# Making the low part of every second half block of the up projection with ScalarE and an accumulating transfer

## The chip, the cores and the metric

The kernel runs on one core of a Trainium2 chip. Its engines are TensorE (PE; PEld is its weight load), VectorE (DVE), ScalarE (ACT), GpSimd (POOL) and SyncE (SP, which issues most transfers). The metric is the time of one execution in microseconds (us) as the device measures it, the median of several runs; lower is better.

## The reference

Two layers of an encoder on 256 tokens of width 2048, all in float32. What this change touches is the gated feed-forward part:

```python
h2 = rms_norm(x, ln2_g[l])
u = depthwise_conv(h2 @ w_up[l], conv_w[l], conv_b[l])     # w_up: 2048 x 11264
gate, up = u[..., :D_FF], u[..., D_FF:]                    # D_FF = 5632
x = x + (jax.nn.silu(gate) * up) @ w_down[l]
```

Before it each layer has an input projection, two attention groups and an output projection.

## The kernel before

Float32 products are made from parts. Each weight tile `w` and each activation is split into a high part `hi`, which is `w` rounded to the matmul's float32r type, and a low part `lo = w - hi`. For the up projection `two` issues for each block of 128 rows of weights one matmul of 512 columns (the high part of the weights times both parts of the activation, whose parts lie side by side) and one of 256 columns (the low part of the weights times the high part of the activation).

All weights come in blocks of 1 MB, the *quanta*: 128 partitions x 2048 floats. `load` fetches a block into one of three buffers `raw`, by a transfer on SP's queue. Each block is worked off in two halves of 128 x 1024, the *steps* `(q, half)`. `split_w(s)` takes a pair of buffers `whi`, `wlo` (five of each: SPLIT_AHEAD = 4, plus one) and calls `split`: ACT copies the half block to `whi` with rounding (L104), VectorE subtracts it from the original into `wlo` (L105). The main loop, for each step, splits the weights of four steps ahead and then issues the step's matmuls (L86). When both halves of a block are split, its `raw` buffer is given up and the load of the block three further on is issued.

A layer has 36 blocks of the input projection, 16 of the output projection, and in the feed-forward part 88 blocks of the up projection (two for each of 44 column blocks `f`) and 44 of the down projection. Up and down alternate: the up projection of 13 column blocks, then the down projection over 12 of them, then 12 more, and so on (CHUNKS). After the second block of an `f`, `glu` runs: ACT takes half of the result out of PSUM (L505), VectorE adds the other half and scales it into `halo` (L506, L507), POOL copies the edges of `halo` (L509, L510), ACT and VectorE do the conv of width 3 (L515, L517), ACT the SiLU (L519), VectorE the product (L520), and the split of the result into `mid`.

The order of instructions on each engine isn't written out by hand. A scheduler orders what the program records by priorities and by its own reckoning of times; `tc.high_priority` lets the splits go ahead of other work. The queues of the engines then run strictly in that order, with semaphores between them.

`lo` in a second half of the up projection is thus made by L105 on VectorE as everywhere else; POOL issues no transfers, and in the up projection it has only the two halo copies of each `f`.

Of the kernel before, what the change touches and what calls it, by code (L numbers as in the profile page):

```python
# [11 lines left out]
F32 = mybir.dt.float32  # L12
F32R = mybir.dt.float32r
I32 = mybir.dt.int32
AF = mybir.ActivationFunctionType
ALU = mybir.AluOpType
# [27 lines left out]
AHEAD_PRIO = 40  # L44
# [7 lines left out]
def encoder_kernel(  # L52
# [5 lines left out]
    nc = tc.nc  # L58
# [42 lines left out]
    def split(hi, lo, src, scale=None):  # L101

        if scale is None:
            high = nc.scalar.activation(hi, src, AF.Copy)  # L104
            nc.vector.tensor_sub(lo, src, hi.bitcast(F32))  # L105
        else:
            high = nc.scalar.activation(hi, src, AF.Copy, scale=scale)  # L107
            nc.vector.scalar_tensor_tensor(lo, src, scale, hi.bitcast(F32),
                                           op0=ALU.mult, op1=ALU.subtract)
        return high  # L110
# [266 lines left out]
    quanta = []  # L377
# [199 lines left out]
    raw, hl, left, loads, highs = {}, {}, {}, {}, {}  # L577

    def load(q, parts=1):
        if q < len(quanta):  # L580
            raw[q] = wp.tile([P, 2048], F32, name="raw", bufs=3)
            left[q] = 2
            m = 2048 // parts
            for j in range(parts):
                loads[q] = nc.sync.dma_start(out=raw[q][:, j * m:(j + 1) * m], in_=quanta[q][0][:, j * m:(j + 1) * m])

    def split_w(s, parts=1):
        if s < len(steps):
            q, half = steps[s]
            at_ = UP_AT if quanta[q][2] else 0  # L590
            hl[s] = tuple(wp.tile([P, 1024 + 64], F32R, name=t, bufs=SPLIT_AHEAD + 1)[:, at_:at_ + 1024]
                          for t in ("whi", "wlo"))
            m = 1024 // parts
            for j in range(parts):
                with tc.high_priority(offset=AHEAD_PRIO if s >= KD // 2 else 0):
                    highs[s] = split(*(t[:, j * m:(j + 1) * m] for t in hl[s]),
                                     raw[q][:, half * 1024 + j * m:half * 1024 + (j + 1) * m])
            left[q] -= 1
            if left[q] == 0:
                del raw[q]  # L600
                load(q + LOAD_AHEAD)
# [61 lines left out]
    for i in range(SPLIT_AHEAD):  # L663
        first_x(i)
        split_w(i, 2 if i == 0 else 1)
# [14 lines left out]
    for s, (q, half) in enumerate(steps):  # L680
        if s + SPLIT_AHEAD < KD // 2:
            first_x(s + SPLIT_AHEAD)
        split_w(s + SPLIT_AHEAD)
        quanta[q][1](q, half, *hl.pop(s))
        for f, args in side.pop((q, half), []):
            f(*args)
# [83 lines left out]
```

## Time and profile before

| | |
|---|---|
| time, median of 3 runs | 2126.05 us (2126.02 to 2126.58) |
| the profiled execution's own time | 2126.1 us |
| its span in the trace | 2124.3 us |
| granted TensorE clock | 1.00 |
| mean transfer rate over the span | 187 GB/s, 397.89 MB |

The profile is one execution. A group's row names the source line, the engine, the operation, the tile written and the tiles read, the shape and the number of instructions; behind the bar stand busy time in us, the mean of one in ns, and the idle time of the engine just before them with what ended most of it. A row of the timeline has the start in us, the duration in us, the engine and the operation, and in brackets the idle time before it. In the windows each engine's busy time stands in the order PE, PEld, DVE, ACT, POOL, and then the granted clock, the busy share of the DMA engines and GB/s.

### The profile page before, as it was taken

Reading aid. Unit: us, or ns where it says so; the run is one execution under the profiler, and the core shown is the slowest. Engines: PE = TensorE matmul, PEld = TensorE weight load, DVE = VectorE, ACT = ScalarE, POOL = GpSimd, SP = SyncE. Lnnn points to the kernel's source line nnn. Section 1 sums busy time; section 2 is a strip of 40 time slices with the busy share of each in tenths; the row PEclk is TensorE's granted clock in tenths of the full one; section 3 lists DMA queues with packets and bytes.
Section 4 is the critical chain, followed back from the end, with each engine's and each line's share of the span. In section 5 each row is a group of like instructions: output and inputs, shape, how many; then the busy total and the mean of one; then the engine's idle time right before and its main releaser. Section 6 shows DMA issues by size and latency. Waiting matters only on the chain.

```text
span 2124.3 us, 28802 instructions
## 1 busy us (share of the span) xinstructions
PE 2118.1 (100%) x10904; PEld 1815.3 (85%) x10904; DVE 1458.0 (69%) x2293; ACT 1141.2 (54%) x1651; POOL 142.1 (7%) x215
## 2 busy tenths in 40 slices
PE   9999999999999999999999999999999999999999
PEld 8888888888888888888888888888888888888887
DVE  7777667775677577657756866677756775776575
ACT  7566556554455355535655665565544553555453
POOL 0000000110011011001000000001100100110010
PEclk9999999999999999999999999999999999999999
DMA  9544555555555555555555454555555555555554
GB/s 345 195 141 170 176 178 178 181 197 198 181 196 191 189 195 182 196 198 182 196 180 197 139 171 160 174 182 185 197 194 184 195 188 192 193 185 197 192 185 139
DMA packets 60843, 397.89 MB, mean 187 GB/s; under 512 B 7328, under 2 KB 9888, under 8 KB 13728
## 3 DMA queue, kind: packets, MB, share of 16 engines
q1 hardware_dynamic: 59696, 394.71, 54.3%
q8 instruction: 85, 1.39, 0.3%
q10 hardware_dynamic: 1008, 1.34, 0.2%
q14 instruction: 54, 0.44, 0.1%
HBM read 393.93 MB, written 2.10 MB: 186 GB/s over the span
## 4 chain that ended last, share of the span: by engine, by line
PE 99%; DMA 0%; ACT 0%; DVE 0%; ACTq 0%; DVEq 0%; issue 0%
PE mm L86 95%; PE pv L86 1%; PE S L86 1%; PE tr L292 1%; PE S L140 0%; PE tr L353 0%; PE tr L86 0%; DMA ln_g<-in_ln_g 0%; PE tr L348 0%; PE tr L345 0%; DVE x L546 0%; ACT xs L107 0%; ACT whi L104 0%; ACTq L608 0%; DVEq L765 0%
## 5 line engine op out<-in xcount | busy, mean ns | idle before, releaser
L105 DVE TENSOR_TENSOR wlo<-raw,whi 128x1024 fp32r<-128x1024 f32 (+1 forms) x737 | 901.2, 1223 | 543.8 <-ACT whi L104 504.9
L104 ACT ACTIVATE whi<-raw 128x1024 fp32r<-128x1024 f32 (+1 forms) x737 | 779.7, 1059 | 863.1 <-PE mm L86 671.9
L86 PE MATMUL mm<-xs,whi 128*128 128x512 f32 x2816 | 976.6, 390 | 0.0
L86 PE MATMUL mm<-xs,wlo 128*128 128x256 f32 x2816 | 794.1, 282 | 0.0
L86 PEld LDWEIGHTS mm<-xs,whi 128*128 128x128 f32 x2816 | 528.3, 188 | 110.5
L86 PEld LDWEIGHTS mm<-xs,wlo 128*128 128x128 f32 x2816 | 532.2, 189 | 0.8
L86 PE MATMUL mm<-whi,mid 128*128 128x512 f32 x1920 | 481.5, 391 | 0.0
L86 PEld LDWEIGHTS mm<-whi,mid 128*128 128x128 f32 x1920 | 357.9, 188 | 72.7
L86 PE MATMUL mm<-whi,xs 128*128 128x512 f32 x1152 | 296.3, 395 | 0.7 <-ACT whi L104 0.7
L86 PE MATMUL mm<-wlo,mid 128*128 128x512 f32 x960 | 260.0, 390 | 0.0
L86 PEld LDWEIGHTS mm<-whi,xs 128*128 128x128 f32 x1152 | 214.6, 188 | 45.4 <-ACT whi L104 1.4
L86 PEld LDWEIGHTS mm<-wlo,mid 128*128 128x128 f32 x960 | 180.0, 188 | 37.2
L86 PE MATMUL mm<-wlo,xs 128*128 128x512 f32 x576 | 162.0, 396 | 0.0
L517 DVE SCALAR_TENSOR_TENSOR pT<-halo,conv,pT 128x256 f32<-128x256 f32 x352 | 146.7, 479 | 0.5
L86 PEld LDWEIGHTS mm<-wlo,xs 128*128 128x128 f32 x576 | 107.3, 188 | 21.7 <-DVE wlo L105 0.4
L509 POOL COPY halo<-halo 128x6 f32<-128x6 f32 x88 | 22.7, 258 | 1359.8 <-DVE halo L507 1359.8
L515 ACT ACTIVATE pT<-halo,conv 128x256 f32<-128x256 f32 x176 | 95.1, 588 | 0.2
L510 POOL COPY halo<-halo 128x6 f32<-128x6 f32 x88 | 95.1, 1081 | 0.2 <-POOL halo L509 0.2
L507 DVE TENSOR_TENSOR halo<-prob,r 128x512 f32<-128x512 f32 x88 | 60.9, 692 | 2.7
L506 DVE TENSOR_TENSOR prob<-prob,mm 128x512 f32<-128x512 f32 x88 | 59.9, 681 | 0.0
L453 DVE TENSOR_TENSOR x<-x,mm 128x1024 f32<-128x1024 f32 x28 | 34.2, 1221 | 35.3 <-PE mm L86 35.3
L505 ACT ACTIVATE prob<-mm 128x512 f32<-128x512 f32 x88 | 51.1, 581 | 0.0
(129 smaller groups left out, 857.8 us busy)
## 6 DMA issues: line engine op xcount, KB each, us to landing
raw<-in_w_up SPq DMA_DIRECT2D x176, 1024.0 KB, 4.8
raw<-in_w_down SPq DMA_DIRECT2D x88, 1024.0 KB, 4.8
raw<-in_w_in SPq DMA_DIRECT2D x71, 1024.0 KB, 4.9
raw<-in_w_out SPq DMA_DIRECT2D x32, 1024.0 KB, 4.8
bias<-in_bias SPq DMA_DIRECT2D x16, 160.0 KB, 3.8
x<-in_x SPq DMA_DIRECT2D x4, 512.0 KB, 8.9
out<-x SPq DMA_DIRECT2D x6, 256.0 KB, 2.5
mid<-in_xT ACTq DMA_DIRECT2D x4, 256.0 KB, 6.2
```

The lines of the kernel that those rows point to most:

```text
L86: nc.tensor.matmul(ps, lhsT, rhs, start=start, stop=stop, skip_group_check=True)
L104: high = nc.scalar.activation(hi, src, AF.Copy)
L105: nc.vector.tensor_sub(lo, src, hi.bitcast(F32))
L292: nc.tensor.transpose(ps[:, j, tt * P:(tt + 1) * P], qn[tt][:, p + j, :], ident)
L453: nc.vector.tensor_add(xv, xv, ps)
L505: nc.scalar.activation(t, ps[:, :, 0], AF.Copy)
L506: nc.vector.tensor_add(t, t, ps[:, :, 1])
L507: nc.vector.tensor_mul(ux[:, :, r:r + T], t, st["r2"][:, None, :].to_broadcast([P, 2, T]))
L509: nc.gpsimd.tensor_copy(ux[:, :, 1:r], ux[:, :, T:T + r - 1])
L510: nc.gpsimd.tensor_copy(ux[:, :, T + r:T + 2 * r - 1], ux[:, :, r + 1:2 * r])
L515: nc.scalar.activation(y[:, j, :], ux[:, j, r:r + T], AF.Identity, scale=w1, bias=b)
L517: nc.vector.scalar_tensor_tensor(y[:, j, :], ux[:, j, o:o + T], w, y[:, j, :], op0=ALU.mult, op1=ALU.add)
```

## The change

In `split_w`, for the second half (`half == 1`) of each block of the up projection, ACT makes the high part as before (now L599), then writes its negative into `lo` (L600), and POOL issues a transfer that reads the same half block of the weights a second time from memory and adds it to `lo` (L601). VectorE's subtraction is left out for these half blocks; the first halves and all other weights are split as before. Lines behind the insertion have numbers that are 9 higher.

```diff
             m = 1024 // parts
+            if quanta[q][2] and half == 1:
+
+                hi, lo = hl[s]
+                w = raw[q][:, 1024:2048]
+                with tc.high_priority(offset=AHEAD_PRIO):
+                    highs[s] = nc.scalar.activation(hi, w, AF.Copy)
+                    nc.scalar.activation(lo, hi.bitcast(F32), AF.Copy, scale=-1.0)
+                    nc.gpsimd.dma_start(out=lo, in_=quanta[q][0][:, 1024:2048], accum_op=ALU.add)
+                parts = 0
             for j in range(parts):
```

On ACT, in the middle of the first up projection, one turn of an `f` (`whi` and `wlo` are the parts of the weights, `prob`, `pT` and `mid` tiles of `glu`) stood before as

```order
L505 ACTIVATE prob<-mm 128x512
L104 ACTIVATE whi<-raw 128x1024
L515 ACTIVATE pT<-halo_110,conv 128x256 x2
L104 ACTIVATE whi<-raw 128x1024
L519 ACTIVATE prob<-pT 128x256
L104 ACTIVATE whi<-raw 128x1024
L104 ACTIVATE mid<-prob 128x256
L104 ACTIVATE whi<-raw 128x1024
```

and stands now as

```order
L505 ACTIVATE prob<-mm 128x512
L599 ACTIVATE whi<-raw 128x1024
L600 ACTIVATE wlo<-whi 128x1024
L515 ACTIVATE pT<-halo_110,conv 128x256 x2
L104 ACTIVATE whi<-raw 128x1024
L519 ACTIVATE prob<-pT 128x256
L599 ACTIVATE whi<-raw 128x1024
L104 ACTIVATE mid<-prob 128x256
L600 ACTIVATE wlo<-whi 128x1024
L104 ACTIVATE whi<-raw 128x1024
```

Two copies were put in, one ahead of the conv's L515, the other behind the split of `glu`'s result.

On POOL, in the same place, only halo copies stood one behind the other before; the rows now are

```order
L601 DMA wlo<-in_w_up 128x1024 x2
L509 COPY halo_110<-halo_110 128x2x3
L510 COPY halo_110<-halo_110 128x2x3
L601 DMA wlo<-in_w_up 128x1024 x2
L509 COPY halo_112<-halo_112 128x2x3
L510 COPY halo_112<-halo_112 128x2x3
```

Two transfers stand between the halo copies of one `f` and of the next.

On PE the order differs only at the start of the up projection of each layer (`pv<-tq,ones` is the matmul that spreads the norm's factor `r2`; the numbers behind `xs` tell the activation tiles apart). Before:

```order
L86 MATMUL mm<-xs_2796,whi 128x512
L86 MATMUL mm<-xs_2796,wlo 128x256
L86 MATMUL mm<-xs_2799,whi 128x512
L86 MATMUL mm<-xs_3091,whi 128x512
L86 MATMUL mm<-xs_3091,wlo 128x256
L86 MATMUL mm<-xs_2799,wlo 128x256
L86 MATMUL mm<-xs_2807,whi 128x512
L86 MATMUL mm<-xs_2807,wlo 128x256
L86 MATMUL mm<-xs_2810,whi 128x512
L86 MATMUL mm<-xs_2810,wlo 128x256
L86 MATMUL mm<-xs_2796,whi 128x512
L86 MATMUL pv<-tq,ones 128x256
```

and now:

```order
L86 MATMUL mm<-xs_2796,whi 128x512
L86 MATMUL mm<-xs_2796,wlo 128x256
L86 MATMUL pv<-tq,ones 128x256
L86 MATMUL mm<-xs_3093,whi 128x512
L86 MATMUL mm<-xs_3093,wlo 128x256
```

The matmul into `pv` moved ahead of nine others; the same matmuls follow in a slightly different order. SP's order of transfers is unchanged.

## The prediction

> **What bounds the kernel now.** I read the page first: busy time by engine, then the chain that ended last, then the costliest groups.
>
> ```profile
> span 2124.3 us, 28802 instructions
> PE 2118.1 (100%) x10904; PEld 1815.3 (85%) x10904; DVE 1458.0 (69%) x2293; ACT 1141.2 (54%) x1651; POOL 142.1 (7%) x215
> ...
> PE 99%; DMA 0%; ACT 0%; DVE 0%; ACTq 0%; DVEq 0%; issue 0%
> ...
> L105 DVE TENSOR_TENSOR wlo<-raw,whi 128x1024 fp32r<-128x1024 f32 (+1 forms) x737 | 901.2, 1223 | 543.8 <-ACT whi L104 504.9
> L104 ACT ACTIVATE whi<-raw 128x1024 fp32r<-128x1024 f32 (+1 forms) x737 | 779.7, 1059 | 863.1 <-PE mm L86 671.9
> L86 PE MATMUL mm<-xs,whi 128*128 128x512 f32 x2816 | 976.6, 390 | 0.0
> L86 PE MATMUL mm<-xs,wlo 128*128 128x256 f32 x2816 | 794.1, 282 | 0.0
> ```
>
> PE is busy all the time, makes 99% of the chain, and its two groups of the up projection have 0.0 us of idle time before them. VectorE's group is the second largest of the page, but it stood idle 504.9 us waiting for ACT's high part, and ACT 671.9 us waiting for PE to give a buffer back. So both helpers wait for PE, never the other way round. A busy PE need not be a PE at its pace, so I looked at the starts of its matmuls in an undisturbed stretch of the up projection (timeline, PE alone, first and last 128x512 row; 86 pairs lie between them):
>
> ```profile
> 559.90 0.39 PE L86 MATMUL mm<-xs,whi 128*128 128x512 f32 x1
> ...
> 589.72 0.39 PE L86 MATMUL mm<-xs,whi 128*128 128x512 f32 x1
> ```
>
> 29.82 us / 86 = 346.7 ns for each pair, without a gap. A half block has 8 pairs: one step is 2.77 us, and a pair of steps (one 1 MB block of weights) is 5.55 us. None of these matmuls is removed, so there is nothing to win below this pace. The whole question is whether a wait appears in PE.
>
> **The lead that a low part has.** There are five buffers of `whi` and `wlo` (SPLIT_AHEAD + 1). The pair that step s-1 gives back is filled for step s+4, and PE runs four steps in between: 4 x 2.77 = 11.1 us. The timeline shows ACT, POOL and VectorE in one turn of it:
>
> ```profile
> 569.40 1.06 ACT L104 ACTIVATE whi<-raw 128x1024 fp32r<-128x1024 f32 x1 [1.24 <-PE mm L86]
> 570.37 1.08 ACT L515 ACTIVATE pT<-halo,conv 128x256 f32<-128x256 f32 x2
> 572.17 1.06 ACT L104 ACTIVATE whi<-raw 128x1024 fp32r<-128x1024 f32 x1 [0.71 <-ACT pT L515]
> 573.13 0.40 ACT L519 ACTIVATE prob<-pT 128x256 f32<-128x256 f32 x1
> 574.95 1.06 ACT L104 ACTIVATE whi<-raw 128x1024 fp32r<-128x1024 f32 x1 [1.42 <-PE mm L86]
> 575.91 0.40 ACT L104 ACTIVATE mid<-prob 128x256 fp32r<-128x256 f32 x1
> ...
> 570.39 0.19 POOL L509 COPY halo<-halo 128x6 f32<-128x6 f32 x1 [9.77 <-DVE halo L507]
> 570.51 1.26 POOL L510 COPY halo<-halo 128x6 f32<-128x6 f32 x1
> ...
> 570.50 1.23 DVE L105 TENSOR_TENSOR wlo<-raw,whi 128x1024 fp32r<-128x1024 f32 x1 [0.24 <-ACT whi L104]
> 571.64 1.67 DVE L517 SCALAR_TENSOR_TENSOR pT<-halo,conv,pT 128x256 f32<-128x256 f32 x4
> ```
>
> ACT starts the high part as PE gives the buffer back (569.40, 1.24 us waited for PE), VectorE's low part is done at 570.50 + 1.23 = 571.73. PE asks for it 11.1 us after the release, at about 580.3: some 8.6 us to spare.
>
> **The change, part by part.** There are 176 blocks of the up projection, so 176 second halves.
>
> VectorE: 176 x 1.223 = 215 us less. It waits for ACT and nothing on PE's path waits for it: worth 0.
>
> ACT: 176 more copies of a 128x1024 tile. ACT has no such SBUF copy apart from L104, so 1.059 us each: 186 us more, off the path. Per 50 us of the up projection (9 second halves) ACT rises from the 28.30 us of the window below to 28.3 + 9 x 1.06 = 37.8 us. Behind the new copy stand the two L515 of the conv, moved back by 1.06 us, and the next high part: 569.40 + 1.06 + 1.06 + 1.08 = 572.6 and some tenths for hand-overs, so 0.5 to 0.7 us late against 572.17. It has 8 us to spare: 0. The conv's result is wanted by the down projection only, and one block of `f` is computed ahead of it; VectorE, with 1.23 us less to do in that turn, gives the delay back: 0.
>
> Order of release: `raw` loses VectorE as reader of its second half. Loads on SP wait for that reader today, so they go out about 1.2 us earlier, and into the same time as the new transfer. SP's own order is unchanged.
>
> ```profile
> SPq L585 <- DVE wlo L105: 1328.7, 253, 7.7
> ...
> raw<-in_w_up SPq DMA_DIRECT2D x176, 1024.0 KB, 4.8
> ...
> x<-in_x SPq DMA_DIRECT2D x4, 512.0 KB, 8.9
> out<-x SPq DMA_DIRECT2D x6, 256.0 KB, 2.5
> ...
> 10.00:30.00 20.00, 19.98 (x88) 16.09 (x87) 18.64 (x42) 15.37 (x28) 0.00 (x0) 1.00 1.03 400
> 400.00:450.00 50.00, 50.00 (x291) 44.34 (x290) 37.76 (x54) 28.30 (x41) 5.68 (x10) 1.00 0.56 190
> ```
>
> (SP's waits; issues with KB and us to landing; windows, whose last three numbers are granted clock, DMA share and GB/s.)
>
> POOL: 176 issues. The trace has no transfer issued by POOL. Lower bound 0; upper bound the longest thing POOL does in this phase, 1.26 us, which is a copy that ran from end to end beside VectorE's 1.23 us L105 (the copy before it took 0.19). I take 1.26 us. The halo copies stand between the issues; they come at 570.39, before the new ACT copy is done (571.5), so neither holds up the other by more than that.
>
> The accumulating transfer: 512 KB, none in the trace. From below, 2.5 us (256 KB to memory, alone); from above, 8.9 us (512 KB, in the crowded start, where the window shows 400 GB/s). The nearest is the 1 MB load at 4.8 us under this very phase's load: it moves as many bytes as 512 KB that is read from memory plus 512 KB that is read back from the tile. I take 4.8.
>
> The sum for a second half: the high part and the copy, 2 x 1.06 with 0.2 us of hand-overs, are done 2.3 us after the start at 569.40; in the other second half of a turn `mid` stands between, 0.4 us more: 2.7. Of the 10.9 us from that start to PE's demand 8.2 us are left. Issue 1.26 + landing 4.8 = 6.1 us. It fits with 2.1 us to spare; with the upper bounds, 1.26 + 8.9 = 10.2, it is 2.0 us late.
>
> The Trainium skill (DMA: Bandwidth & Descriptors, the anatomy of a DMA issued by GpSimd) gives about 2.0 us plus bytes over 436 GB/s for such a transfer, by estimate 3.2 us here; by that the slack would be 5 us minus the issue. No run here shows one yet.
>
> Start of each up projection: PE's order differs there alone; the little matmul behind `r2` comes 9 matmuls, about 1.5 us, earlier, and the chain to it on VectorE has lost one L105 of 1.23 us. At most 0.3 us twice, and at best nothing: 0.
>
> Sum: 2124.3 us span + 1.8 us around it (the profiled run took 2126.1) + 0 = 2126.1 us; the median of the runs is 2126.05. A change within 0.2% (4.3 us) I call the same.
>
> **Rivals.**
>
> *The low part lands late (slower).* Place: the first `wlo` matmul of a second half. It decides from a landing of 8.2 - 1.26 = 6.9 us after issue. A late half block also delays the releases behind it, and the four steps of the lead hold two second halves, so each loses half of the lateness: 0.7 us late costs 176 x 0.35 = 62 us, 2188 us; the bound of 2.0 us late costs 176 us, 2302 us. For it: 512 KB has taken 8.9 us once the queues were full, and the earlier raw load will run beside it. Against: raw loads in this phase land in 4.8 us with twice the bytes.
>
> *The DMA engines run out (slower).* The share in the up projection is 0.56 at 190 GB/s; the new bytes are half as many, 95 GB/s. If an accumulated byte costs one passage, the share is 0.84; if two, 1.12 (in bytes, 380 GB/s); if three, 1.40. The most this trace shows is 1.03 at 400 GB/s. Two passages are thus just inside by bytes and 9% over by share: 0.5 us per block. `raw` has three buffers and about 9 us of slack (five steps of 2.77 less a 4.8 us landing) per up phase, and the phases have 26, 24, 24 and 14 blocks: (4 + 3 + 3) x 2 layers = 20 us, 2146 us. Three passages are 36% over, 2.0 us per block: (52 + 48 + 48 + 28 - 36) x 2 = 280 us, 2406 us.
> The Trainium skill (DMA: Bandwidth & Descriptors, rules for kernel authors) says that an accumulate reads its destination and writes it later, which is a second read and so the two-passage case; what that costs per byte it does not say, and no run here shows it yet.
>
> *POOL or ACT becomes the wait (slower).* An issue far longer than 1.26 us, with the halo copies queued behind it, would hold up the conv; it decides only when POOL's two issues and copies exceed a turn of 11.1 us, so over 4.8 us for each issue: 2 x 5 + 1.45 = 11.5 us, 0.4 us for 88 turns, 35 us, 2161 us.
> The Trainium skill (SBUF — State Buffer, who interferes with whom) says that a VectorE instruction with two SBUF inputs contends with GpSimd reading SBUF; the 1.26 us copy beside L105 agrees.
>
> *Faster.* VectorE's 215 us would have to stand on the path somewhere. PE's groups with 0.0 us of idle time speak against it; all that lies outside PE is 2124.3 - 2118.1 = 6.2 us, at start and end. If all went, 2120 us.
>
> **Numbers.** Same 0.50. Late landing 0.22, DMA engines 0.21, POOL or ACT 0.04: slower 0.47. Faster 0.03. The likeliest is no change, 2126.1 us; its own range is 2123 to 2130. The range has to reach into the slower cases: the late landing up to 2260 and the two-passage case lie inside; left out are the upper end of the late landing (0.04) and most of the three-passage case (0.12). Low end 2122.
>
> **What would show it.** Right: PE 100% and pairs 346.7 ns apart, VectorE near 1458 - 215 = 1243 us, ACT near 1328 us, DMA share in the up projection 0.84 to 1.0, landings of the new transfer under 6.9 us, ACT's high part still waiting for PE. Wrong: PE idle time before `mm<-xs,wlo` released by a DMA into `wlo` (late landing); ACT waiting for `raw`, with raw loads landing far later than 4.8 us (DMA engines); L515 or L517 waiting for POOL (third rival). The number that I know least is what an accumulated byte costs; it alone can make the forecast wrong by more than a few us.

## The result and the profile after

The changed kernel took 2153.87 us (median, 2150.56 to 2157.5) against 2126.27 us for the kernel before in the same session: a ratio of 1.013 with an interval of 1.011 to 1.015. It is slower by 27.6 us. The profiled execution took 2157.5 us with a span of 2155.7 us, 31.4 us more than the span before; the lines below are from it.

From its page: the busy time by engine, the chain that ended last by engine, the queue of the new transfers (packets, MB, share of the 16 engines' span), the costliest groups, and the issues with their KB and us to landing.

```profile
span 2155.7 us, 29105 instructions
PE 2128.2 (99%) x10904; PEld 1815.0 (84%) x10904; DVE 1255.3 (58%) x2117; ACT 1318.0 (61%) x1827; POOL 221.5 (10%) x391
...
q0 software_dynamic: 25344, 92.29, 23.8%
...
PE 78%; DMA 13%; issue 5%; DVE 2%; ACT 2%; POOL 0%; POOLq 0%; ACTq 0%; DVEq 0%
...
L86 PE MATMUL mm<-xs,wlo 128*128 128x256 f32 x2816 | 798.5, 284 | 20.4 <-DMA wlo<-in_w_up 19.9
L86 PEld LDWEIGHTS mm<-xs,wlo 128*128 128x128 f32 x2816 | 532.3, 189 | 33.2 <-DMA wlo<-in_w_up 32.0
L601 POOL DMA_DIRECT2D wlo<-in_w_up x176 | 153.3, 871 | 977.3 <-ACT wlo L600 967.8
...
raw<-in_w_up SPq DMA_DIRECT2D x176, 1024.0 KB, 7.2
wlo<-in_w_up POOLq DMA_DIRECT2D x176, 512.0 KB, 8.2
```

The chain was PE for 99%; now the transfer into `wlo` holds 13% of it. PE's low-part matmuls had 0.0 us of idle time before them; now their weight loads stand idle 32.0 us for the DMA into `wlo`. That is close to the 31.4 us by which the span grew. The landing of the new transfer, counted from the start of POOL's issue, is 8.2 us in the median, and the raw loads of the up projection have gone from 4.8 to 7.2 us. VectorE and ACT stand near the 1243 and 1328 us forecast: 1255.3 and 1318.0 us.

The view of the tile `wlo` gives the range of that landing:

```profile
DMA to landing us min/median/max: 5.5/8.2/10.6
```

Even the shortest is longer than the 4.8 us of a raw load before. A window of 90 us in the first up projection (busy time of PE, PEld, DVE, ACT, POOL; then granted clock, DMA share, GB/s):

```profile
360.00:450.00 90.00, 86.47 (x492) 75.38 (x491) 48.50 (x80) 64.61 (x87) 15.54 (x31) 1.00 1.00 269
```

PE stands still 3.5 us of 90. The DMA engines have a packet under way all the time, at 269 GB/s; at the start of the kernel before they moved 400 GB/s at a share of 1.03. So they are taken up by fewer bytes per second than they have moved elsewhere.

The chain in the same place, in order of time (start, us, what):

```profile
401.61 0.45 ACT whi L599
402.06 0.52 issue
402.57 0.15 ACT mid L104
402.72 0.16 issue
402.88 1.05 ACT wlo L600
403.93 0.39 issue
404.33 10.13 DMA wlo<-in_w_up
414.46 0.04 issue
414.50 11.04 PE mm L86 x62
```

The same turn from the timeline, with ACT, SP, POOL and PE's weight load:

```profile
401.61 1.06 ACT L599 ACTIVATE whi<-raw 128x1024 fp32r<-128x1024 f32 x1 [1.04 <-PE mm L86]
...
402.69 0.33 SPq L585 DMA_DIRECT2D raw<-in_w_up  x1
402.88 1.04 ACT L600 ACTIVATE wlo<-whi 128x1024 fp32r<-128x1024 f32 x1
...
404.33 0.86 POOL L601 DMA_DIRECT2D wlo<-in_w_up  x1 [4.83 <-ACT wlo L600]
...
414.50 0.19 PEld L86 LDWEIGHTS mm<-xs,wlo 128*128 128x128 f32 x1 [1.80 <-DMA wlo<-in_w_up]
```

This is the prediction's sum, read off: ACT's start at 401.61, the copies done 2.3 us later, the issue at 404.33 (2.72 us after the start), a landing of 10.13 us, and PE, which wanted the half block at about 412.7, waits 1.80 us. The row to keep in mind is SP's: at 402.69, as soon as ACT's high part has read `raw`, a 1 MB load is issued, 1.64 us ahead of the transfer. In the kernel before that load waited for VectorE and had the engines to itself.

### The profile page after: what moved, and what is told of

Its sections match the earlier page's. It is cut to its first block, busy times and chain, and to the rows that moved or that the text cites. A ratio compares the mean times of both kernels' runs of the same rounds, so it can differ in the third digit from the quotient of the medians.

```text
span 2155.7 us, 29105 instructions
## 1 busy us (share of the span) xinstructions
PE 2128.2 (99%) x10904; PEld 1815.0 (84%) x10904; DVE 1255.3 (58%) x2117; ACT 1318.0 (61%) x1827; POOL 221.5 (10%) x391
## 3 DMA queue, kind: packets, MB, share of 16 engines
q0 software_dynamic: 25344, 92.29, 23.8%
## 4 chain that ended last, share of the span: by engine, by line
PE 78%; DMA 13%; issue 5%; DVE 2%; ACT 2%; POOL 0%; POOLq 0%; ACTq 0%; DVEq 0%
PE mm L86 74%; DMA wlo<-in_w_up 13%; PE pv L86 1%; PE S L86 1%; DVE wlo L105 1%; ACT whi L104 1%; ACT wlo L600 1%; PE tr L292 1%; DVE halo L507 1%; PE S L140 0%; DVE prob L506 0%; PE tr L353 0%; ACT whi L599 0%; PE tr L86 0%; DMA ln_g<-in_ln_g 0%
## 5 line engine op out<-in xcount | busy, mean ns | idle before, releaser
L105 DVE TENSOR_TENSOR wlo<-raw,whi 128x1024 fp32r<-128x1024 f32 (+1 forms) x561 | 684.6, 1221 | 540.5 <-ACT whi L104 504.1
L104 ACT ACTIVATE whi<-raw 128x1024 fp32r<-128x1024 f32 (+1 forms) x561 | 591.9, 1057 | 503.8 <-PE mm L86 465.8
L599 ACT ACTIVATE whi<-raw 128x1024 fp32r<-128x1024 f32 x176 | 186.6, 1060 | 215.1 <-PE mm L86 215.0
L601 POOL DMA_DIRECT2D wlo<-in_w_up x176 | 153.3, 871 | 977.3 <-ACT wlo L600 967.8
L600 ACT ACTIVATE wlo<-whi 128x1024 fp32r<-128x1024 f32 x176 | 185.4, 1053 | 3.3 <-ACT whi L599 0.2
L515 ACT ACTIVATE pT<-halo,conv 128x256 f32<-128x256 f32 x176 | 95.0, 587 | 0.0
L105 DVE TENSOR_TENSOR mid<-prob,mid 128x256 fp32r<-128x256 f32 x88 | 37.3, 424 | 81.4 <-ACT mid L104 81.4
```

Source lines behind the costliest of these rows:

```text
L515: nc.scalar.activation(y[:, j, :], ux[:, j, r:r + T], AF.Identity, scale=w1, bias=b)
L599: highs[s] = nc.scalar.activation(hi, w, AF.Copy)
L600: nc.scalar.activation(lo, hi.bitcast(F32), AF.Copy, scale=-1.0)
L601: nc.gpsimd.dma_start(out=lo, in_=quanta[q][0][:, 1024:2048], accum_op=ALU.add)
```

## The experiments

Three causes were open. **T**: an accumulated byte costs more than one passage, the DMA engines run out, and the order of the transfers is of no matter. **L** (called Q in later expectations): the engines would do, but the load that goes out ahead holds up the transfer, which has no slack, while the load has much. The third: ACT's 176 copies or the new order cost the time. All edits are to the changed kernel's lines L599 to L601 and were timed against the kernel before on the same chip (medians 2126.12 to 2126.22).

The next table is worked out from the single transfer records of the traces. A packet here is one such record; each transfer into `wlo` has 128 with data and 16 of 4 bytes, its completions. The times are medians over the 176 transfers (88 in `only_u1`), in us after ACT's start on the half block. "Late" counts the transfers whose last completion came more than 10.9 us after that start, when PE asks for the half block by the prediction's sum. "Busy" is an estimate of what the packets of one block need of each of the 16 DMA engines, as a share of PE's 5.55 us per block: 8 raw packets of 309 ns, and 8 of the low part (328 ns for 4 KB that are added, 253 for 3 KB, 178 for 2 KB, 174 for 4 KB not added); for `only_u1` it is the mean of its two kinds of block. These are median packets, which ran undisturbed. With the mean packets of the changed kernel (370 and 362 ns), which contain the time that they held each other up, its share is 106% and not 92%. The DMA share that the profile shows for the window 360:450 is higher too: 1.00 in the changed kernel, 0.97 in `short768`, 0.90 in `short512`, 0.86 in `plain`, 0.83 in `only_u1`.

| kernel | load issued | transfer issued | first packet | last packet | late | busy | time, us |
|---|---|---|---|---|---|---|---|
| changed | 1.09 | 2.56 | 5.54 | 10.37 | 54 of 176 | 92% | 2153.9 |
| loadlate | 2.27 | 2.56 | 7.05 | 12.35 | 150 | 92% | 2269.1 |
| lofirst | 2.03 | 2.41 | 6.71 | 12.09 | 144 | 92% | 2290.7 |
| lofirst2 | 2.03 | 1.47 | 3.98 | 10.43 | 94 | 92% | 2172.0 |
| loadafter | 3.71 | 2.56 | 4.39 | 8.44 | 25 | 92% | 2142.8 |
| cols768 | 1.55 | 2.35 | 6.07 | 10.69 | 68 | 81% | 2176.3 |
| short768 | 1.09 | 2.56 | 5.29 | 9.99 | 21 | 81% | 2140.7 |
| loadafter768 | 3.50 | 2.35 | 4.00 | 7.75 | 21 | 81% | 2138.9 |
| short512 | 1.09 | 2.56 | 5.14 | 7.33 | 0 | 70% | 2126.3 |
| plain | 1.09 | 2.56 | 5.14 | 7.52 | 0 | 70% | 2126.4 |
| only_u1 | 1.09 | 2.72 | 5.18 | 8.74 | 0 of 88 | 68% | 2126.6 |

### ACT's copies without the transfer

```diff
-  nc.gpsimd.dma_start(out=lo, in_=quanta[q][0][:, 1024:2048], accum_op=ALU.add)
+  nc.vector.tensor_add(lo, w, lo.bitcast(F32))
```

> ACT writes the high part and its negative as in the changed kernel, but VectorE adds the loaded block to the low part and there is no transfer. It tells what ACT's 176 extra copies and the changed order cost by themselves. All theories that put the loss on the transfer: 2125.5 to 2127 us. If ACT's copies or the later conv cost part of it: 2130 us or more.

Measured 2126.27 us, ratio 1.000 (0.9991 to 1.001). Its page:

```profile
PE 2118.0 (100%) x10904; PEld 1815.3 (85%) x10904; DVE 1460.5 (69%) x2293; ACT 1327.0 (62%) x1827; POOL 71.8 (3%) x215
```

ACT does the 186 us more and PE is at 100%. The copies and their place in ACT's order cost nothing: the third cause is out.

### The same transfer without the addition

```diff
-  nc.gpsimd.dma_start(out=lo, in_=quanta[q][0][:, 1024:2048], accum_op=ALU.add)
+  nc.gpsimd.dma_start(out=lo, in_=quanta[q][0][:, 1024:2048])
```

> As the changed kernel, but the transfer from GpSimd overwrites the low part instead of adding to it (the low part then holds the weights, so the result leaves the subtraction out). Bytes from memory, issue and queue stay. Theory T: an accumulated byte costs two passages, so a plain 512 KB takes about 1.5 us of the engines: 4.4 to 4.6 us per block, share about 0.8, no wait of PE: 2126 to 2129 us. If what is slow is a transfer issued by GpSimd as such (issue, latency, small packets), landing stays near 8 us and the time near 2150 us.

Measured 2126.36 us, ratio 1.0001 (0.9991 to 1.001). Its page, the queue and the landing:

```profile
q0 software_dynamic: 25344, 92.29, 13.0%
...
wlo<-in_w_up POOLq DMA_DIRECT2D x176, 512.0 KB, 5.2
```

The window, as above:

```profile
360.00:450.00 90.00, 90.00 (x521) 79.81 (x520) 50.68 (x83) 67.89 (x90) 11.27 (x34) 1.00 0.86 285
```

The same bytes at the same moment behind the same load, moved and not added, land in 5.2 us, and PE is busy 90.00 of 90 us, at more GB/s than in the changed kernel. This is the time that T expected. So the second reading of the weights and the load ahead are affordable; what makes them dear here is the addition. (POOL's issue is shorter here, 0.53 us against 0.87; `short512` below has the long one and loses nothing.) The price of the addition stands in the rows of q0: 23.8% x 16 x 2155.7 us / 25344 = 324 ns for a mean packet, against 13.0% x 16 x 2124.4 / 25344 = 174 ns. An added byte costs 1.9 times a moved one in these packets.

### The load put later, still ahead of the transfer

```diff
-  nc.scalar.activation(lo, hi.bitcast(F32), AF.Copy, scale=-1.0)
+  neg = nc.scalar.activation(lo, hi.bitcast(F32), AF.Copy, scale=-1.0)
   nc.gpsimd.dma_start(out=lo, in_=quanta[q][0][:, 1024:2048], accum_op=ALU.add)
+  with tc.issue_after(neg.ins):
+      nc.scalar.activation(work.tile([P, 1], F32, name="late", bufs=2), w[:, 0:1], AF.Copy)
```

> As the changed kernel, same bytes, same order of ACT's copies, but ACT reads one column of the loaded block behind its negative, so that SP's 1 MB load goes out about 2.3 us after ACT's start on the half block (1.09 before) and 0.3 us before the transfer's issue (1.47 before). Theory Q (the transfer comes behind whatever load is set off ahead of it, and lands about 9 to 10 us after that load's issue): last packet at 11.5 to 12.5 us after ACT's start instead of 10.4, more than 120 of 176 transfers past PE's 10.9 us, 2230 to 2300 us. Theory T (the engines are full, the order does not matter): 2150 to 2162 us.

Measured 2269.05 us, ratio 1.0669 (1.0654 to 1.0685). The timeline of one turn:

```profile
401.14 1.06 ACT L599 ACTIVATE whi<-raw 128x1024 fp32r<-128x1024 f32 x1 [1.25 <-PE mm L86]
...
403.20 0.18 ACT L603 ACTIVATE late<-raw 128x1 f32<-128x1 f32 x1
...
403.41 0.33 SPq L585 DMA_DIRECT2D raw<-in_w_up  x1
403.70 0.87 POOL L601 DMA_DIRECT2D wlo<-in_w_up  x1 [1.28 <-ACT late L603]
```

Its page, the landings:

```profile
raw<-in_w_up SPq DMA_DIRECT2D x176, 1024.0 KB, 9.3
wlo<-in_w_up POOLq DMA_DIRECT2D x176, 512.0 KB, 10.2
```

PE's waits (us in total, times, longest):

```profile
PEld mm L86 <- DMA wlo<-in_w_up: 114.7, 66, 3.6
```

The same transfers, the same bytes, POOL's issue as long after ACT's start as before; only the load goes out 1.2 us later, 0.3 us ahead of the transfer (403.41 and 403.70). It costs another 115 us, as L expected. T, for which order does not matter, falls here. A part of the 115 us is PE's clock, as the last section shows. The table shows why: in every row whose load went out ahead, the first packet of the transfer came 4.0 to 4.8 us after the issue of that load (5.54 - 1.09 = 4.45, 7.05 - 2.27 = 4.78, 5.14 - 1.09 = 4.05), however long after its own. By then 0.84 to 0.98 MB of the load had been started in the records. The load goes first nearly as a whole, so a later load makes a later low part.

The Trainium skill (DMA: Bandwidth & Descriptors, queues, rings and completion order) says that each DMA engine goes round robin over the queues that have work, and drains a whole packet of one, typically 9 to 17 descriptors, before it switches. What the Trainium skill calls a packet is thus a group of single moves, where a packet of the table is one record of the trace. A load has 128 records of 8 KB, 8 for each of the 16 engines; if those 8 make one packet in the other sense, the rule agrees with a load that goes first nearly as a whole. Where such a packet ends these records do not show.

### The load put behind the transfer

```diff
-  nc.gpsimd.dma_start(out=lo, in_=quanta[q][0][:, 1024:2048], accum_op=ALU.add)
+  add = nc.gpsimd.dma_start(out=lo, in_=quanta[q][0][:, 1024:2048], accum_op=ALU.add)
+  with tc.issue_after(add.ins):
+      nc.gpsimd.tensor_copy(work.tile([P, 1], F32, name="late", bufs=2), w[:, 0:1])
```

> As the changed kernel, but GpSimd reads one column of the loaded block right behind each accumulating transfer's issue, so SP's next 1 MB load goes out about 1 us after that issue instead of 1.5 us before it. Theory Q (the accumulating transfer stands behind the load that the same release sets off: in the changed kernel its first packet comes 4.4 us after the load's issue, when 0.84 MB of the load has started, and so it did in the 768-column kernel, 4.5 us, and in the one with the low part first, 4.7 us): its first packet comes 2.5 to 3.2 us after its own issue, landing falls from 8.2 to 5.5 to 7 us, the load lands later within its 9 us of slack, PE's waits nearly vanish: 2126 to 2132 us. Theory T (the engines are full): same bytes, same time, 2145 to 2160 us.

Measured 2142.8 us, ratio 1.009 (1.006 to 1.0119). The timeline of one turn:

```profile
403.00 0.86 POOL L601 DMA_DIRECT2D wlo<-in_w_up  x1 [4.58 <-ACT wlo L600]
...
403.55 0.51 POOL L603 COPY late<-raw 128x1 f32<-128x1 f32 x1
404.08 0.33 SPq L585 DMA_DIRECT2D raw<-in_w_up  x1
```

Its page, the landings:

```profile
raw<-in_w_up SPq DMA_DIRECT2D x176, 1024.0 KB, 7.5
wlo<-in_w_up POOLq DMA_DIRECT2D x176, 512.0 KB, 6.4
```

With the load 1.1 us behind the transfer instead of 1.6 us ahead, the landing falls from 8.2 to 6.4 us and 11 of the 27.6 us come back, at the same bytes. Order counts, but 16.6 us stay: order alone is not the whole cause, and both expectations missed. Here 25 transfers still land late although the median lands some 2 us early. A transfer has landed when the last of its 16 completions is in. In these late ones the 16th comes 1.9 us (median) after the 15th; in the changed kernel's late ones 0.92 us after it, and only 14 of its 54 would have been late by the 15th. If each completion stands for one DMA engine, which the records do not say, a single engine lags; which one and why is open.

### The negative made first

```diff
-  highs[s] = nc.scalar.activation(hi, w, AF.Copy)
-  nc.scalar.activation(lo, hi.bitcast(F32), AF.Copy, scale=-1.0)
+  nc.scalar.activation(lo, w, AF.Copy, scale=-1.0)
   nc.gpsimd.dma_start(out=lo, in_=quanta[q][0][:, 1024:2048], accum_op=ALU.add)
+  highs[s] = nc.scalar.activation(hi, w, AF.Copy)
```

> ACT writes the negative of the rounded weights into the low part directly from the loaded block and before the high part, so the transfer is issued about 1.1 to 1.5 us earlier after PE's release. Theory T (the 16 DMA engines are full: per block 2.97 us for the load plus 2.9 us for the accumulation, 5.9 us against PE's 5.55): the lead is won once per up phase and then used up, so of the 27.6 us lost at most 8 x 1.1 to 1.5 = 9 to 12 us come back: 2141 to 2146 us, DMA share in the middle of a phase still about 1.0. Theory L (the chain after the release is about 1 us too long for the four steps of lead, the engines only look full): the waits of up to 2.1 us shrink to almost nothing: 2126 to 2131 us.

Measured 2290.69 us, ratio 1.0763 (1.0723 to 1.0802): both missed, since the edit did not do what it was meant to. The scheduler still put the high part first, and as both copies now read `raw`, the load went out at 2.03 us, 0.38 us ahead of the transfer. It is much the case of `loadlate`, reached by another way. Its page, the landing:

```profile
wlo<-in_w_up POOLq DMA_DIRECT2D x176, 512.0 KB, 10.3
```

PE's waits:

```profile
PEld mm L86 <- DMA wlo<-in_w_up: 123.6, 61, 4.2
```

`lofirst2` forces the order with `issue_after`, as in `loadlate`, the high part behind the negative: now the transfer goes out at 1.47 us and the load 0.56 us behind it.

> ACT is held to write the negative into the low part before it makes the high part (in the first kernel of that idea the high part still came first and both delayed the load to 0.4 us before the transfer's issue). The transfer is issued about 1.3 us after PE's release instead of 2.6, and the load, which waits for the high part, about 1 us behind it. Theory Q: transfer ahead of the load and 1.3 us more lead: landing 5.5 to 7 us, PE's waits vanish, 2126 to 2129 us. Theory T (the engines are full): 2141 to 2150 us.

Measured 2171.99 us, ratio 1.0214 (1.0194 to 1.0234): again both missed. Its page, the landings:

```profile
raw<-in_w_up SPq DMA_DIRECT2D x176, 1024.0 KB, 9.2
wlo<-in_w_up POOLq DMA_DIRECT2D x176, 512.0 KB, 9.9
```

The first packet came early, at 3.98 us, but then the load ran beside the transfer all the way: from first to last packet it took 6.4 us, against 4.1 us in `loadafter`, whose load came 1.15 us behind the issue. Going first by half a microsecond is not enough.

### Fewer added bytes

`cols768` makes 768 of the 1024 columns by the negative and the transfer and lets VectorE subtract the other 256:

```diff
-  nc.scalar.activation(lo, hi.bitcast(F32), AF.Copy, scale=-1.0)
-  nc.gpsimd.dma_start(out=lo, in_=quanta[q][0][:, 1024:2048], accum_op=ALU.add)
+  nc.scalar.activation(lo[:, 0:768], hi[:, 0:768].bitcast(F32), AF.Copy, scale=-1.0)
+  nc.gpsimd.dma_start(out=lo[:, 0:768], in_=quanta[q][0][:, 1024:1024 + 768], accum_op=ALU.add)
+  nc.vector.tensor_sub(lo[:, 768:1024], w[:, 768:1024], hi[:, 768:1024].bitcast(F32))
```

> Only the first 768 of the 1024 columns of each second half are made by ACT's negative and the transfer, the other 256 by VectorE; number of transfers and their place are unchanged. Theory T: 2.97 + 0.75 x 2.9 = 5.15 us per block, below 5.55: share about 0.93, PE's waits vanish, 2126 to 2129 us. Theory L: the landing shortens by a quarter of its data time (0.7 us) of about 8.2 and ACT's copy by 0.25 us; waits of up to 2.1 us shrink to about half: 2133 to 2142 us.

Measured 2176.32 us, ratio 1.0253 (1.0192 to 1.0313): a quarter fewer added bytes, both expectations missed, and 22 us slower than the change. VectorE reads `raw` again, so the load goes out at 1.55 us instead of 1.09, and the first packet comes 0.53 us later. This too speaks against T.

`short768` and `short512` keep every instruction of the change and the load at 1.09 us, and only narrow the transfer (`lo[:, 0:768]` or `lo[:, 0:512]`, and as many columns of the weights).

> As the changed kernel in everything but the transfer's length: it adds only the first 768 columns; the low part of the other 256 is left as ACT's negative, so the result leaves that addition out. The load goes out 1.09 us after ACT's start as in the changed kernel (the 768-column kernel before set it off at 1.55, since VectorE read the block too). Theory Q with the amount as second factor: last packet at 9.3 to 9.8 us after ACT's start, few past 10.9, 2126 to 2134 us. If the place of the load does not matter: like the 768-column kernel, 2168 to 2185 us.

> As the changed kernel in everything but the transfer's length: it adds only the first 512 columns (256 KB); the low part of the other 512 is left as ACT's negative, so the result leaves that addition out. Still 176 transfers, the load 1.09 us after ACT's start and ahead of them. If the amount that the 16 DMA engines carry makes the late ones (1024 columns: 27.6 us lost, 768: 14.5 us), the last of the 16 lands at about 8 to 9 us after ACT's start, no PE wait, 2126 to 2130 us, like the kernel with half as many transfers (2126.6). If a straggling engine comes with each transfer of this kind whatever its size: 2132 to 2140 us.

Measured 2140.7 us (1.0066, 1.0052 to 1.008) and 2126.33 us (1.0002, 0.9992 to 1.0012). The window of the first:

```profile
360.00:450.00 90.00, 89.65 (x516) 79.03 (x515) 50.44 (x83) 67.07 (x89) 16.40 (x32) 1.00 0.97 258
```

And of the second:

```profile
360.00:450.00 90.00, 90.00 (x521) 79.78 (x520) 50.64 (x83) 67.91 (x90) 16.72 (x34) 1.00 0.90 237
```

With 1024, 768 and 512 added columns and the load ahead in all three, the loss is 27.6, 14.5 and 0.2 us. At 768 the expectation of L was too low and the other far too high; at 512 the number of those for whom the amount decides was met: the load still goes first (first packet 5.14 us), and nothing is lost, since what follows takes 2.2 us instead of 4.8.

`loadafter768` joins both remedies, the load behind the transfer and the 768 columns of `cols768`:

> Both remedies: the transfer covers 768 of 1024 columns (VectorE subtracts the rest) and the load is issued behind it, by GpSimd's read of one column. If order and amount together make the loss (Q with engines at 92% of their time in the full kernel, 81% here): first packet 4.4 us after ACT's start, last 7.5 to 8.5, no more than a few late, 2126 to 2129 us. If the order alone matters and what is left in the full kernel with the load behind (17 us) has another cause: 2138 to 2145 us.

Measured 2138.89 us, ratio 1.0057 (1.0042 to 1.0071), which is the second of the two numbers: what is left with the load behind does not go away with a quarter fewer added bytes (16.6 us lost in `loadafter`, 12.7 here). Its page, the landing:

```profile
wlo<-in_w_up POOLq DMA_DIRECT2D x176, 384.0 KB, 5.6
```

PE's waits:

```profile
PEld mm L86 <- DMA wlo<-in_w_up: 11.6, 16, 1.6
```

A median landing of 5.6 us leaves 3 us of slack, and still 21 transfers land late; by the 15th completion 3 of them would. The median does not decide, the last engine of the worst transfers does.

`only_u1` treats only the second of the two blocks of each `f` the new way (`ups[q]` is 1 for it), so 88 full transfers:

```diff
-  if quanta[q][2] and half == 1:
+  if quanta[q][2] and half == 1 and ups[q] == 1:
```

> Only the second block of each column block is made the new way: 88 transfers instead of 176. Theory T (the engines are full): the mean load falls well below full, 2126 to 2128 us. Theory Q: each transfer that is left still stands behind its load; these 88 are the ones where the split of the conv's result stands between ACT's two copies, which gave PE's waits in the changed kernel, but no accumulation precedes the load any more: landing 7 to 8 us and a quarter to a half of the loss, 2132 to 2142 us.

Measured 2126.58 us, ratio 1.0003 (0.9993 to 1.0012). Its page, the raw loads:

```profile
raw<-in_w_up SPq DMA_DIRECT2D x176, 1024.0 KB, 5.0
```

These transfers are the same as in the changed kernel, with the load 1.6 us ahead; there 25 of these 88 were late (of all 176, 54), here none is. What differs is the block between, in which the engines have nothing to add. The load ahead alone does no harm (L's number missed, and T's, which goes by the mean load of the engines, was met); it does when the engines are nearly full.

### The addend from the raw buffer

`in_=w` adds the half block from `raw` in SBUF instead of reading it from memory again; it was to tell whether the second reading from memory is what costs.

> The transfer adds the loaded block in SBUF instead of reading the weights from memory again; the buffer of the load is then held until the transfer lands. Theory T (the engines' passages are what is full, wherever the bytes come from): accumulating packets as long as before, share about 1.0 in the up phases though memory traffic falls to 190 GB/s, time 2140 to 2165 us. Rival H (memory reads are what is full): share falls towards 0.7, landing to 5 to 6 us, 2126 to 2130 us.

Measured 2244.6 us, ratio 1.0555 (1.0535 to 1.0576). ACT's waits:

```profile
ACT whi L104 <- DMA raw<-in_w_up: 254.0, 99, 5.2
```

Both expectations missed, and the edit brought a wait of its own: `raw` is now held until the transfer lands, its next load goes out late, and ACT waits 254.0 us for raw blocks, which neither kernel shows in the up projection. The added packets took 328 ns as before, which speaks for the addition and against the source; but the time of this run answers another question, and how memory and SBUF share in the cost stays open.

## Why the prediction was right and where it failed

The forecast of 2126.1 us, no change, missed by 27.8 us; the range (2122 to 2260) held the time only because it was drawn wide enough for the rivals. The case called likeliest (no change, 0.50) did not come, so the forecast's own mechanism failed in one term of its sum, the landing of the transfer.

- **PE bounds, and VectorE's 215 us are worth nothing**: right. `short512` and `plain` relieve VectorE, `actonly` does not, and all stand at 2126.3 to 2126.4 us.
- **ACT's 186 us and its order are worth nothing**: right, shown by `actonly`.
- **POOL's issue**, bounded by 0 and 1.26 us and taken as 1.26: 0.871 us. The sum subtracted it from the slack, but the landing is counted from the start of the issue, as the chain shows (404.33 + 10.13 = 414.46). So the point of decision was a landing of about 8.3 us, not 6.9. POOL as a wait, the third rival, is out: the same 176 issues cost nothing in `short512`.
- **The landing of 4.8 us: this term failed.** It measured 8.2 us in the median and 10.6 us at most (the bounds were 2.5 and 8.9). It was taken from a raw load, on the ground that the bytes moved are as many. Those loads had the engines to themselves and add nothing; the transfer adds, and stands behind one of them. Its first packet comes 3 us after the issue, and its packets need 4.8 us from first to last, against 2.4 us in `plain`, where the same transfer behind the same load landed in 5.2 us. The 3.2 us that stood beside the sum as an estimate was further off still: the shortest landing was 5.5 us.
- **The loads that go out 1.2 us earlier, into the same time as the transfer**: the prediction named it and gave it no term in the sum. It costs a good half of the 3.4 us by which the landing was taken too low: with the load put behind (`loadafter`) the landing falls by 1.8 us, and the first packet comes 1.8 us after the issue instead of 3. The prediction watched the slack of the load, some 9 us, and not that of the transfer, which by its own sum was 2.1 us.
- **The DMA engines at two passages**: 1.9 measured, the right case. But the forecast was a share of 1.12 and then loads falling behind. The undisturbed packets need 92% of PE's pace, the window shows a share of 1.00, and ACT never waited for a raw block of the up projection. The load had the slack and gave it; the low part paid.
- **The late landing as a rival**: right in place (PE's weight load of `wlo`, released by the DMA). Its price took every half block to be equally late (0.7 us: 2188 us). In fact 54 of 176 landed late, PE's weight loads waited 38 times, and the waits came to 32.0 us.

So the cause was neither rival alone. Shown by the runs: the addition fills the engines (`plain`, `short512` and `only_u1`, at 68 to 70% by undisturbed packets, lose nothing), and at 92% the order in which load and transfer are issued moves the time between 2142.8 and 2290.7 us at equal bytes. Not settled: which completion comes last and why, why 12.7 us stay in `loadafter768`, and why `lofirst` costs 22 us more than `loadlate`, whose load goes out later; some 8 us of these are PE's clock. No version was faster than the kernel before; PE was already busy throughout.

## What to carry to other kernels

When a step is moved from an engine to a transfer, ask first which other transfers the same release sets off, and which of them has the slack: the one with slack should be issued last, by a full microsecond and not by half of one. Count an accumulating transfer as two, and leave the DMA engines room (here 70% by undisturbed packets cost nothing, 81% did; nothing between was tried): a transfer is as late as the last of its 16 completions, so the median landing does not tell whether someone will wait. A duration from a transfer that runs alone is a lower bound for one that runs behind another (4.8 and 8.2 us here).

## What the runs showed of the hardware

An added 4 KB packet takes 328 ns and a moved one 174 (medians, changed kernel and `plain`). The Trainium skill (DMA: Bandwidth & Descriptors, rules for kernel authors) says that an accumulate reads its destination and writes it later; the ratio of 1.9 agrees.

In the runs with the longest waits TensorE's granted clock fell to one half for stretches of 3.4 or 6.8 us: 20 of them in `loadlate` (mean clock 0.984), 24 in `lofirst` (0.980), 12 in `sbufsrc` (0.990), one in `cols768`, and none in the changed kernel, whose longest wait was 2.1 us, or in `loadafter` (2.5 us). The window of `loadlate`, in which the clock is 0.94:

```profile
360.00:450.00 90.00, 81.26 (x437) 70.36 (x437) 42.33 (x70) 58.03 (x90) 14.23 (x28) 0.94 0.92 245
```

Around the start of each stretch PE had stood idle, without matmul or weight load, for 1.8 to 3.8 us; idle times of up to 2.8 us also passed without one. The Trainium skill (TensorE: Matmul & The Clock Gate, part 1) says that the clock is halved after at least one idle window of about 3.4 us. The stretches have that length here, but the idle times that led to them were mostly shorter, so standing idle for 2 us can already be enough. It makes a late transfer dearer: in these stretches the pairs of matmuls are 640 ns apart instead of 347. By estimate that is 33 us of what `loadlate` lost (71.7 us of half clock) and 41 us of what `lofirst` lost (88.7 us).

POOL's second halo copy became faster by the change, from 1081 ns to:

```profile
L510 POOL COPY halo<-halo 128x6 f32<-128x6 f32 x88 | 27.4, 311 | 0.3 <-POOL halo L509 0.2
```

Before, 80 of the 88 copies ran beside a subtraction L105 on VectorE, now 10 do; beside one a copy takes 1.2 to 1.3 us, otherwise 0.18. In `actonly`, where VectorE's addition comes one ACT copy later, the mean is 330 ns as well, so it is the coincidence and not VectorE's total that counts. Nothing on PE's path had waited for it.
